# Block 1: which products TensorE takes while the mixers of a layer run

## The chip, the core and the metric

The kernel runs on one core of one Trainium2 chip. The metric is the device time of one execution in microseconds (us); before the change it is 2,830.08 us, the median of three runs (2,829.87 to 2,831.25). The engines are named as in the profile: PE (TensorE, matmuls) with PEld (its weight loads), DVE (VectorE), ACT (ScalarE), POOL (GpSimd) and SP (which issues the DMAs of the weights). Each engine has a queue of its own and takes its instructions strictly in the order of that queue; across engines they wait for each other by semaphores.

## The reference

One sequence of 512 positions and 1,024 features passes two layers of a first block and two of a second. The change touches the first block alone, and there the mixers:

```
h = rms_norm(x);  y = h @ w_in + b_in        # split in columns: mq mk mv mo mi mf | hq hf hi hg | sq sk sv
m_out = head_norm(mlstm(silu(conv(mq, mk)), mv, mi, mf)) * sigmoid(mo)
h_out = head_norm(hgrn2(hq, hf, hi)) * silu(hg)
s_out = swa_sink_attention(rope(norm(sq)), rope(norm(sk)), sv, sinks)
x = x + concat(m_out, h_out, s_out) @ w_out
x = x + square(relu(rms_norm(x) @ w_up)) @ w_down
x = x + sigmoid(rms_norm(x) @ w_ple_gate) * rms_norm(p @ w_ple_proj)
```

`mlstm` is causal linear attention with exponential gates over 4 heads, `hgrn2` a gated recurrence over 4 heads, `swa_sink_attention` attention over a window of 128 positions with 8 query heads.

## The kernel before, in words

Positions come in four tiles of 128. Every projection is a sum of three products, `hi*hi + hi*lo + lo*hi`, of operands split into two fp32r parts (`mm3`, L176 to L178). I call these "products" below. A product for a position-major group has 256 columns, one for a feature-major group or for the output projection 512. Weights come by DMA into `wr`, ACT casts them to `wh`, DVE subtracts to get `wl` (L136, L137).

A layer's mixers are written in this order in `mixers1`: projections of the attention; the attention (`swa`, four tiles of four pairs of heads); projections for HGRN2 (`feat(0)`, `feat(1)`, `w_hi1`) and for the mLSTM (`w_mv1`; `feat(2)` and `feat(3)`, both from `w_f1`); HGRN2 and the mLSTM; the gates (`w_hg1`, `w_mo1`); then the output projection in three parts, `w_oa1` for the attention's rows, `w_oh1` for HGRN2's, `w_ob1` for the mLSTM's.

That is not the order in which an engine gets them. A scheduler gives each engine the instruction that it takes to be ready first and, among those, the one written earlier; so products that need only the normed input are pulled forward into every gap that the scheduler sees on PE. Inside the stages the following runs on PE besides the products, all in plain fp32:

- attention, per pair of heads: two score matmuls (`score_pair`, L1088; the first waits by an added dependency for the mask-and-max operation that read the pair before), then on DVE the mask and maximum (L583, L585), on ACT an exponential for each head (L586), on PE transposes (L591), on ACT a copy (L594), on PE the product with the values (L598);
- HGRN2: eight levels; DVE computes decays and multiplies (L707 to L716), PE does 32 small matmuls a level (L728 for level 0, L732 for the others), DVE merges the result (`copy_predicated`, L739). Level 7 needs no decay;
- mLSTM, per head: four score matmuls (L855), ACT exponentials (L858, L860), DVE multiplies (L862), and ten matmuls with the values (L867).

After a group of products a sink reads its PSUM bank: for the gates L486 (DVE), for the output projection the add into `x` at L497 (DVE), for `feat` L419 (DVE) and L420 (ACT). Banks for products rotate over three buffers.

Of the kernel before, what the change touches and what calls it, by code (L numbers as in the profile page):

```python
# [61 lines left out]
class Builder:  # L62
    def __init__(self, ctx, tc, d, out, cfg=None):
        self.tc, self.nc, self.d, self.out = tc, tc.nc, d, out
        self.cfg = cfg or {}
        nc = self.nc
# [5 lines left out]
        self.nmm, self.banks, self.late = 0, ("mm",), None  # L72
        self.pend, self.nstart, self.sread = [], 0, None
        xa = cp.tile([P, NF * S], F32, name="x")
# [316 lines left out]
    def mixers1(self, l, mp, act, nxt):  # L391
        nc = self.nc
# [70 lines left out]
        self.tok_group(w, 8, 264, act, mv_sink)  # L463
        feat(2)
        feat(3)
        ctx = ExitStack()
# [13 lines left out]
        for name, off, dst, silu in (("w_hg1", O_HG, gg, True), ("w_mo1", O_MO, gm, False)):  # L480
            w = self.wload(name, l, 8 * 256)
            b = bias(off, 256)

            def gate_sink(t, pt, b=b, dst=dst, silu=silu):
                z = dst[t]
                nc.vector.scalar_tensor_tensor(z, pt, rt[:, t:t + 1], b, ALU.mult, ALU.add)  # L486
                th = self.tmp()[:, 0:256]
                nc.scalar.activation(th, z, AF.Tanh, scale=0.5)
                if silu:
                    nc.vector.scalar_tensor_tensor(th, th, 1.0, z, ALU.add, ALU.mult)  # L490
                    nc.vector.tensor_tensor(z, th, gh[:, 256:512], ALU.mult)
                else:
                    nc.vector.scalar_tensor_tensor(z, th, 1.0, gh[:, 0:256], ALU.add, ALU.mult)
            self.tok_group(w, 8, 256, act, gate_sink)

# [27 lines left out]
    def swa(self, l, mp, sp, ysw, row):  # L523
        nc, tc = self.nc, self.tc
        o = 512
        gq, gk, sinks = row[:, o:o + 64], row[:, o + 64:o + 128], row[:, o + 128:o + 136]
        gqk = sp.tile([P, 64], F32, name="gqk")
        nc.vector.tensor_tensor(gqk, gq, gk, ALU.mult)
# [39 lines left out]
        for t in range(NT):  # L568
# [9 lines left out]
            for j in range(8):  # L578
                f, c1 = j // 2, slice(j, j + 1)
                if j % 2 == 0:  # L580
                    pts = self.score_pair([(qs[f][u:u + 64, tt], qs[4][u:u + 64, k0:k0 + w], None) for u in (0, 64)], w)
                s = sp.tile([P, 256], F32, name="sw_s", tag="sw_s", bufs=3)[:, :w]
                i = nc.vector.tensor_tensor_reduce(s, pts[j % 2], msk, 1.0, -3.0e38, ALU.add, ALU.max, accum_out=mx[:, c1])  # L583
                self.sread = i.ins if hasattr(i, "ins") else i
                nc.vector.scalar_tensor_tensor(mx[:, c1], mx[:, c1], n8[:, c1], nsk[:, c1], ALU.mult, ALU.min)  # L585
# [21 lines left out]
    def hgrn(self, l, mp, yf, yhi):  # L607
        nc = self.nc
# [87 lines left out]
        for lev in range(8):  # L696
# [23 lines left out]
            for hh in range(2):  # L720
                b = hh * 64
                pt = self.ps("S")
                for i in range(2):
                    kk, qq = ops[i]
                    for c in range(NT):
                        o, u = i * 256 + c * 64, c * P
                        if lev == 0:
                            nc.tensor.matmul(pt[0:64, o:o + 64], kk[b:b + 64, u:u + 64], qq[b:b + 64, u + 64:u + 128],  # L728
                                             start=True, stop=True, tile_position=(b, 0))
                            continue  # L730
                        for r in (0, 64):
                            nc.tensor.matmul(pt[r:r + 64, o:o + 64], kk[b:b + 64, u + r:u + r + 64],  # L732
                                             qq[b:b + 64, u + r:u + r + 64], start=True, stop=True, tile_position=(b, r))
                if lev == 0:
# [45 lines left out]
    def mlstm(self, l, mp, sp, yf, yv, yg, fv, fb):  # L780
# [61 lines left out]
        for h in range(4):  # L842
# [8 lines left out]
            for j in range(NT):  # L851
                w = S - j * P
                js = slice(j * P, j * P + P)
                pt = self.ps("ST"[j % 2])[:, :w]
                nc.tensor.matmul(pt, k[b:b + 64, js], q[b:b + 64, j * P:S], start=True, stop=True)  # L855
                W = sp.tile([P, S], F32, name="ml_W", tag="ml_W", bufs=2)[:, :w]
# [226 lines left out]
    def score_pair(self, qk, ws):  # L1083

        nc = self.nc
        pts = [self.ps("S")[:, :ws] for _ in range(2)]
        for u, (q, k, row) in enumerate(qk):
            i = nc.tensor.matmul(pts[u], q, k, start=True, stop=True, tile_position=None if row is None else (row, 0))  # L1088
            if not u and self.sread is not None:
                self.tc.add_manual_dep(i.ins if hasattr(i, "ins") else i, self.sread.name, SYNC, reason="pair")  # L1090
        return pts

    def softmax_pair(self, mp, qk, t, in1s, scale):
# [5 lines left out]
        for pt, in1 in zip(pts, in1s):  # L1099
            s = mp.tile([P, S], F32, name="at_s", tag="at_s", bufs=5)[:, :w]  # L1100
            st = mp.tile([P, 2], F32, name="at_st", tag="at_st", bufs=8)
            i = nc.vector.tensor_tensor_reduce(s, pt, in1, -scale, 3.0e38, ALU.add, ALU.min, accum_out=st[:, 0:1])
            self.sread = i.ins if hasattr(i, "ins") else i
            nc.scalar.activation(s, s, AF.Exp, bias=st[:, 0:1], scale=-1.0, accum_out=st[:, 1:2])
            out.append((s, st[:, 1:2]))
# [459 lines left out]
```

## Time and profile before

| what | value |
|---|---|
| median of three runs | 2,830.08 us |
| profiled execution, its own time | 2,830.73 us |
| its span, first to last instruction | 2,829.0 us |
| mean granted clock of PE | 0.963 |
| busy: PE, DVE, ACT, POOL | 97%, 63%, 42%, 9% |

The clock is given as a share of full speed: 1.00 is 2.4 GHz and 0.50 is 1.2 GHz. The mixers of layer 0 take roughly the span's first 330 us, those of layer 1 roughly 760 to 1,055 us; the rest of each layer, and the second block, is not touched. Times below are of layer 0 unless layer 1 is named.

### The profile page before, as it was taken

How to read it: one execution, taken by the hardware profiler on the slowest of the kernel's cores; microseconds unless marked ns; L12 is line 12 of the kernel's file. 1: busy time of each engine (PE TensorE's matmuls, PEld its weight loads, DVE VectorE, ACT ScalarE, POOL GpSimd, SP SyncE). 2: the span in 40 equal slices, each digit the busy share in tenths (PEclk: the TensorE clock that was granted, in tenths of full speed). 3: DMA queues.
4: the chain of work that ended last, by engine and by line, in shares of the span. 5: the costliest groups of instructions: out<-in, count | busy, mean ns of one | idle time of the engine just before them, and what ended most of it. 6: DMA issues, size and time to landing. Idle time of an engine off the chain costs nothing.

```text
span 2829.0 us, 42855 instructions
## 1 busy us (share of the span) xinstructions
PE 2735.1 (97%) x16360; PEld 2330.5 (82%) x16360; DVE 1777.3 (63%) x3896; ACT 1189.1 (42%) x2372; POOL 252.5 (9%) x630
## 2 busy tenths in 40 slices
PE   8998999999999899999999999999999899999998
PEld 7876887889987678878988786888889788888887
DVE  6476777558756866774873476755454476665555
ACT  4564432335446434222553555432234554542332
POOL 2000100002200001000031310000001410100000
PEclk9995899999999679999999999999999999999999
DMA  4210277333221105862332211223332312133322
GB/s 152 83 54 30 77 258 256 125 104 105 73 82 65 41 32 179 257 219 97 98 99 92 66 51 58 90 89 101 101 102 72 113 39 85 39 104 97 90 88 77
DMA packets 87644, 285.59 MB, mean 101 GB/s; under 512 B 10972, under 2 KB 15132, under 8 KB 87440
## 3 DMA queue, kind: packets, MB, share of 16 engines
q1 hardware_dynamic: 81280, 266.49, 29.4%
q0 software_dynamic: 5872, 16.35, 2.2%
q8 instruction: 128, 2.10, 0.3%
q14 instruction: 76, 0.62, 0.1%
q10 hardware_dynamic: 288, 0.03, 0.0%
HBM read 280.69 MB, written 2.14 MB: 100 GB/s over the span
## 4 chain that ended last, share of the span: by engine, by line
PE 75%; DVE 10%; DMA 8%; ACT 3%; issue 2%; POOL 2%; SPq 0%; DVEq 0%; ACTq 0%; POOLq 0%
PE ps_mm L176 12%; PE ps_mm L177 12%; PE ps_mm L178 12%; DMA wm<-w_mod 6%; PE ps_T L176 5%; PE ps_T L177 5%; PE ps_T L178 5%; PE ps_S L176 5%; PE ps_S L178 5%; PE ps_S L177 5%; PE ps_S L1088 3%; DVE wm L1031 2%; PE ps_o L1134 1%; PE ps_T L1128 1%; PE ps_T L867 1%
## 5 line engine op out<-in xcount | busy, mean ns | idle before, releaser
L136 ACT CAST wh<-wr 128x1024 fp32r<-128x1024 f32 (+4 forms) x414 | 407.1, 987 | 682.8 <-PE ps_mm L177 247.4
L137 DVE TENSOR_TENSOR wl<-wr,wh 128x1024 fp32r<-128x1024 f32 (+4 forms) x414 | 472.5, 1143 | 306.9 <-ACT wh L136 300.3
L177 PE MATMUL ps_mm<-slotA,wh 128*128 128x512 f32 (+1 forms) x632 | 226.0, 360 | 4.6 <-DVE slotA L137 2.6
L176 PE MATMUL ps_mm<-slotA,wh 128*128 128x512 f32 (+1 forms) x632 | 225.2, 362 | 1.1 <-ACT slotA L316 0.7
L178 PE MATMUL ps_mm<-slotA,wl 128*128 128x512 f32 (+1 forms) x632 | 225.0, 358 | 0.0
L176 PE MATMUL ps_mm<-wh,slotA 128*128 128x256 f32 (+3 forms) x688 | 208.1, 303 | 0.0
L178 PE MATMUL ps_mm<-wh,slotA 128*128 128x256 f32 (+3 forms) x688 | 205.9, 300 | 0.0
L177 PE MATMUL ps_mm<-wl,slotA 128*128 128x256 f32 (+3 forms) x688 | 204.4, 298 | 0.0
L136 ACT CAST m_h<-tmp 128x512 fp32r<-128x512 f32 (+1 forms) x122 | 71.3, 587 | 212.3 <-DVE tmp L910 175.8
L1031 DVE CUSTOM_DVE_ANT_0 wm<-wm,sc 128x1024 f32<-128x1024 f32 x96 | 117.4, 1224 | 68.2 <-DMA wm<-w_mod 67.7
L176 PE MATMUL ps_mm<-slotB,wh 128*128 128x512 f32 (+1 forms) x408 | 141.8, 354 | 4.5 <-ACT slotB L136 3.3
L176 PEld LDWEIGHTS ps_mm<-wh,slotA 128*128 128x128 f32 x688 | 131.6, 192 | 12.2 <-issue 9.5
L177 PEld LDWEIGHTS ps_mm<-slotA,wh 128*128 128x128 f32 x632 | 121.8, 193 | 24.1 <-DVE slotA L137 4.1
L177 PE MATMUL ps_mm<-slotB,wh 128*128 128x512 f32 (+1 forms) x408 | 141.6, 348 | 0.0
L178 PE MATMUL ps_mm<-slotB,wl 128*128 128x512 f32 (+1 forms) x408 | 140.3, 345 | 0.0
L178 PEld LDWEIGHTS ps_mm<-wh,slotA 128*128 128x128 f32 x688 | 131.1, 191 | 7.5 <-issue 6.9
L176 PEld LDWEIGHTS ps_mm<-slotA,wh 128*128 128x128 f32 x632 | 120.8, 193 | 18.3 <-ACT slotA L316 0.9
L178 PEld LDWEIGHTS ps_mm<-slotA,wl 128*128 128x128 f32 x632 | 121.4, 192 | 17.3 <-issue 1.7
L177 PEld LDWEIGHTS ps_mm<-wl,slotA 128*128 128x128 f32 x688 | 131.2, 191 | 5.0 <-issue 4.6
L176 PE MATMUL ps_S<-m_h,wh 128*128 128x512 f32 (+1 forms) x355 | 129.6, 365 | 2.7 <-DVE yacc L944 2.4
L178 PE MATMUL ps_S<-m_h,wl 128*128 128x512 f32 (+1 forms) x355 | 129.2, 364 | 0.0
L177 PE MATMUL ps_S<-m_l,wh 128*128 128x512 f32 (+1 forms) x355 | 129.2, 364 | 0.0
(635 smaller groups left out, 7242.4 us busy)
## 6 DMA issues: line engine op xcount, KB each, us to landing
wr<-w_up SPq DMA_DIRECT2D x152, 512.0 KB, 3.8
wm<-w_mod SPq DMA_DIRECT2D x96, 512.0 KB, 4.6
wr<-w_dn SPq DMA_DIRECT2D x64, 512.0 KB, 4.0
wr<-w_dn SPq DMA_DIRECT2D x32, 384.0 KB, 3.1
wr<-w_dn SPq DMA_DIRECT2D x32, 320.0 KB, 2.8
wr<-w_f SPq DMA_DIRECT2D x16, 512.0 KB, 3.8
wr<-w_pg SPq DMA_DIRECT2D x16, 512.0 KB, 3.8
wr<-w_t SPq DMA_DIRECT2D x12, 512.0 KB, 4.7
```

Source lines behind the costliest of these rows:

```text
L136: nc.scalar.copy(hi, src)
L137: nc.vector.tensor_tensor(lo, src, hi.bitcast(F32), ALU.subtract)
L176: nc.tensor.matmul(out, ah, bh, start=i == 0, stop=False)
L177: nc.tensor.matmul(out, ah, bl, start=False, stop=False)
L178: nc.tensor.matmul(out, al, bh, start=False, stop=i == n - 1)
L867: nc.tensor.matmul(po[:, t * 66:t * 66 + 66], Ps[j][:, (t - j) * P:(t - j) * P + P], yv[j][:, h, :], start=j == 0, stop=j == t)
L1031: nc.vector.tensor_tensor_reduce(w, w, self.sc, 1.0, 0.0, ALU.mult, ALU.add, accum_out=self.mod[l][:, j:j + 1])
L1088: i = nc.tensor.matmul(pts[u], q, k, start=True, stop=True, tile_position=None if row is None else (row, 0))
L1128: nc.tensor.transpose(tp[:, c * P:c * P + P], s[:, c * P:c * P + P], self.ident)
L1134: nc.tensor.matmul(po[u * 64:u * 64 + 64], v(c, u), pT[:, c * P:c * P + P], start=c == 0, stop=c == t, tile_position=(0, u * 64))
```

## The change

Four groups of products get a place in PE's queue behind an instruction of the mixers (an "anchor"), by a context of the framework (`issue_after`): every PE instruction recorded inside it is queued behind the anchor. The anchors are the PE instructions that the diff stores:

- `feat(2)`, `feat(3)` behind the score matmul of the first pair of the attention's last tile;
- the gate of HGRN2 (`w_hg1`) behind the last matmul of level 0, that of the mLSTM (`w_mo1`) behind the last of level 3;
- the first half of `w_oa1` behind level 6, its second half behind the last score matmul of the mLSTM's head 0.

No instruction is added, removed or resized, and no semaphore wait is asked for: the anchor is on the same engine. POOL's and SP's queues keep their order; PE's, DVE's and ACT's change, since the scheduler lays out everything around the new places, and only inside the two layers' mixers.

```diff
-        feat(2)
-        feat(3)
+        for g in (2, 3):
+            with self.tc.issue_after(self.anchor["swa", NT - 1]):
+                feat(g)
...
-            self.tok_group(w, 8, 256, act, gate_sink)
+            with self.tc.issue_after(self.anchor["level", 0 if silu else 3]):
+                self.tok_group(w, 8, 256, act, gate_sink)
...
         for g in range(2):
-            self.feat_group(self.wload("w_oa1", l * 2 + g, 4 * 512), 4, 4, act, sink, 4 * g)
+            with self.tc.issue_after(self.anchor["head", 0] if g else self.anchor["level", 6]):
+                self.feat_group(self.wload("w_oa1", l * 2 + g, 4 * 512), 4, 4, act, sink, 4 * g)
...
+                    self.anchor.setdefault(("swa", t), self.anchor["pair", None])
...
+                            m = nc.tensor.matmul(pt[0:64, o:o + 64], kk[b:b + 64, u:u + 64], qq[b:b + 64, u + 64:u + 128],
+                                                 start=True, stop=True, tile_position=(b, 0))
+                            self.anchor["level", lev] = m.ins
...
+                self.anchor["head", h] = m.ins
...
+            self.anchor["pair", row] = i.ins
```

PE's queue in layer 0 where the attention passes from its tile 1 to tile 2. Before, with the products of `w_f1` (L176 to L178) around the pairs (L1088 scores, L1144 the row that scales a tile's output, L598 values, L591 transposes):

```order
L177 MATMUL ps_mm<-slotA,wh 128x512
L1088 MATMUL ps_S<-sw_q_765,slotB 128x256
L1144 MATMUL ps_T<-ident,tmp 128x128 x4
L1088 MATMUL ps_S<-sw_q_765,slotB 128x256
L598 MATMUL ps_o<-sw_pT,ysw_205 64x128 x2
L598 MATMUL ps_o<-sw_pT,ysw_206 64x128 x2
L591 MATMUL ps_T<-ident,sw_s 128x128 x4
L178 MATMUL ps_mm<-slotA,wl 128x512
```

Now, at the same pairs (lines are 5 to 9 higher):

```order
L1096 MATMUL ps_S<-sw_q_765,slotB 128x256 x2
L603 MATMUL ps_o<-sw_pT,ysw_205 64x128 x2
L603 MATMUL ps_o<-sw_pT,ysw_206 64x128 x2
L1153 MATMUL ps_T<-ident,tmp 128x128 x4
L596 MATMUL ps_T<-ident,sw_s 128x128 x6
L1096 MATMUL ps_S<-sw_q_765,sw_q_751 128x256 x2
L603 MATMUL ps_o<-sw_pT,ysw_206 64x128 x2
L603 MATMUL ps_o<-sw_pT,ysw_207 64x128 x2
L596 MATMUL ps_T<-ident,sw_s 128x128 x2
L1096 MATMUL ps_S<-sw_q_765,sw_q_758 128x256 x2
```

From the last product of `w_mv1` to the anchor no product stands between the pairs any more; the 96 of `w_f1` that stood there, and at the start of the tile after it, all come behind the anchor.

PE's queue in layer 0 from HGRN2's level 3 on. Before, the small matmuls of the levels (L732) follow each other, with a few transposes of the mLSTM (L811, L810) and its first scores (L855):

```order
L178 MATMUL ps_mm<-slotA,wl 128x512
L678 MATMUL ps_o<-yhi_1326,hg_kt_1508 128x128
L732 MATMUL ps_S<-tmp 64x64 x40
L811 MATMUL ps_T<-ident,ml_W 128x4
L810 MATMUL ps_T<-ident,ml_P_1853 128x4
```

Now products of the gates stand between two levels (L738), 32 to 36 at a time:

```order
L176 MATMUL ps_mm<-wh,slotA 128x256
L177 MATMUL ps_mm<-wl,slotA 128x256
L738 MATMUL ps_S<-tmp 64x64 x32
L178 MATMUL ps_mm<-wh,slotA 128x256
L176 MATMUL ps_mm<-wh,slotA 128x256
```

Before, the product that opens the first of these two pieces is the last one ahead of the end of the mLSTM; now all 192 of the two gates and all 96 of `w_oa1` come between level 0 and that end.

DVE's queue in layer 0. Before, the adds of `w_oa1` into `x` (L497) stand among the operations of HGRN2's levels (L715, L716 multiply, L739 merges) and of the mLSTM's gates (L796):

```order
L716 TENSOR_TENSOR tmp<-tmp,slotB 128x8x32
L497 TENSOR_TENSOR x<-x,ps_mm 128x512
L715 TENSOR_TENSOR tmp<-tmp,slotB 128x16x16
L716 TENSOR_TENSOR tmp<-tmp,slotB 128x16x16
L796 SCALAR_TENSOR_TENSOR ml_W<-ml_W 4x512
L137 TENSOR_TENSOR wl<-wr,wh 128x1024
```

Now three of the eight (L499) stand just ahead of the mLSTM's first product of scores and weights (L870), the others behind it:

```order
L838 SCALAR_TENSOR_TENSOR ml_W<-yf_1833,ml_cw,ml_W 128x512 x3
L499 TENSOR_TENSOR x<-x,ps_mm 128x512 x2
L843 SCALAR_TENSOR_TENSOR yf_1833<-ml_W 128x512
L137 TENSOR_TENSOR wl<-wr,wh 128x1024
L499 TENSOR_TENSOR x<-x,ps_mm 128x512
L870 TENSOR_TENSOR ml_P_2313<-ps_S,ml_W 128x512
```

The third of them reads the 36th product of `w_oa1`, so what follows on DVE waits for that.

## Rows read from the trace of the kernel before

**Rows 1.** The page of the profile: its span, and the granted clock in 40 slices.

```profile
span 2829.0 us, 42855 instructions
PEclk9995899999999679999999999999999999999999
```

**Rows 2.** Windows by stage: microseconds, busy time and count per engine, clock, DMA.

```profile
core 0: us, PE busy (x) PEld busy (x) DVE busy (x) ACT busy (x) POOL busy (x), PEclk, DMA share, GB/s
112.20:144.10 31.90, 31.90 (x175) 23.06 (x173) 15.42 (x46) 16.16 (x35) 1.79 (x3) 1.00 0.36 118
144.10:162.60 18.50, 18.50 (x143) 15.20 (x143) 9.25 (x33) 9.75 (x25) 0.00 (x0) 1.00 0.09 30
162.60:249.20 86.60, 75.27 (x763) 61.74 (x761) 79.63 (x176) 48.29 (x88) 6.24 (x11) 0.82 0.17 56
249.20:291.50 42.30, 38.85 (x143) 31.41 (x144) 17.44 (x57) 16.13 (x44) 3.54 (x6) 0.50 0.05 13
949.00:1021.00 72.00, 64.25 (x427) 51.55 (x427) 43.83 (x111) 29.79 (x70) 7.58 (x10) 0.50 0.05 16
```

**Rows 3.** Windows of PE: length, busy (instructions), granted clock, DMA share and GB/s.

```profile
216.00:219.00 3.00, 1.15 (x32) 0.95 0.01 3
219.00:222.00 3.00, 0.43 (x8) 0.50 0.71 208
297.00:300.00 3.00, 2.99 (x16) 0.96 0.00 0
```

**Rows 4.** Timeline of PE: start, length, product; 512 columns, 256 columns, 512 at half clock.

```profile
112.29 0.40 PE L176 MATMUL ps_mm<-slotA,wh 128*128 128x512 f32 x1
112.52 0.39 PE L177 MATMUL ps_mm<-slotA,wh 128*128 128x512 f32 x1
...
157.04 0.28 PE L176 MATMUL ps_mm<-wh,slotA 128*128 128x256 f32 x1
157.16 0.28 PE L177 MATMUL ps_mm<-wl,slotA 128*128 128x256 f32 x1
...
295.55 0.63 PE L176 MATMUL ps_mm<-slotA,wh 128*128 128x512 f32 x1
295.98 0.63 PE L177 MATMUL ps_mm<-slotA,wh 128*128 128x512 f32 x1
```

**Rows 5.** Timeline of PE in the attention: transposes, PV and scores of one pair.

```profile
124.64 0.66 PE L591 MATMUL ps_T<-ident,sw_s 128*128 128x128 f32 x4
...
130.05 0.66 PE L598 MATMUL ps_o<-sw_pT,ysw 128*64 128x128 f32 x8
...
131.00 0.70 PE L1088 MATMUL ps_S<-sw_q,sw_q 64*128 64x256 f32 x4
```

**Rows 6.** Groups by line on ACT, 112.2 to 162.6 us: busy, mean ns, idle before.

```profile
L586 ACT ACTIVATE sw_s<-sw_s,sw_mx,sw_r 128x256 f32<-128x256 f32 x18 | 10.8, 598 | 8.6 <-DVE sw_mx L585 8.6
L594 ACT COPY sw_pT<-ps_T 128x512 f32<-128x512 f32 x8 | 4.7, 582 | 9.9 <-PE ps_T L591 9.9
```

**Rows 7.** Timeline of PE: products of the HGRN2 levels, and the wait before one.

```profile
202.56 0.97 PE L732 MATMUL ps_S<-tmp 64*64 64x64 f32 x32
...
221.57 1.12 PE L732 MATMUL ps_S<-tmp 64*64 64x64 f32 x16 [3.92 <-DVE tmp L716]
...
239.93 1.97 PE L732 MATMUL ps_S<-slotB 64*64 64x64 f32 x32
```

**Rows 8.** Groups by line and form on DVE, 162.6 to 249.2 us.

```profile
L137 DVE TENSOR_TENSOR wl<-wr,wh 128x1024 fp32r<-128x1024 f32 x8 | 9.7, 1218 | 0.1
L497 DVE TENSOR_TENSOR x<-x,ps_mm 128x512 f32<-128x512 f32 x8 | 5.2, 674 | 0.1
L486 DVE SCALAR_TENSOR_TENSOR gg<-ps_mm,rt,brow 128x256 f32<-128x256 f32 x1 | 0.5, 486 | 0.3 <-PE ps_mm L178 0.3
```

**Rows 9.** Timeline of DVE: first operation of HGRN2, first product of the mLSTM.

```profile
162.61 0.64 DVE L634 SCALAR_TENSOR_TENSOR tmp<-slotB 128x512 f32<-128x512 f32 x1
...
249.18 0.69 DVE L862 TENSOR_TENSOR ml_P<-ps_S,ml_W 128x512 f32<-128x512 f32 x1 [1.03 <-ACT ml_W L860]
```

More of the change, by code (lines that the diff above doesn't have):

```diff
@@ L72, in __init__ @@
         self.nmm, self.banks, self.late = 0, ("mm",), None
-        self.pend, self.nstart, self.sread = [], 0, None
+        self.pend, self.nstart, self.sread, self.anchor = [], 0, None, {}
         xa = cp.tile([P, NF * S], F32, name="x")
@@ L526, in swa @@
         gq, gk, sinks = row[:, o:o + 64], row[:, o + 64:o + 128], row[:, o + 128:o + 136]
+        self.anchor = {}
         gqk = sp.tile([P, 64], F32, name="gqk")
@@ L581, in swa @@
                     pts = self.score_pair([(qs[f][u:u + 64, tt], qs[4][u:u + 64, k0:k0 + w], None) for u in (0, 64)], w)
+                    self.anchor.setdefault(("swa", t), self.anchor["pair", None])
                 s = sp.tile([P, 256], F32, name="sw_s", tag="sw_s", bufs=3)[:, :w]
                 i = nc.vector.tensor_tensor_reduce(s, pts[j % 2], msk, 1.0, -3.0e38, ALU.add, ALU.max, accum_out=mx[:, c1])
-                self.sread = i.ins if hasattr(i, "ins") else i
+                self.sread = i.ins
                 nc.vector.scalar_tensor_tensor(mx[:, c1], mx[:, c1], n8[:, c1], nsk[:, c1], ALU.mult, ALU.min)
@@ L727, in hgrn @@
                         if lev == 0:
-                            nc.tensor.matmul(pt[0:64, o:o + 64], kk[b:b + 64, u:u + 64], qq[b:b + 64, u + 64:u + 128],
-                                             start=True, stop=True, tile_position=(b, 0))
+                            m = nc.tensor.matmul(pt[0:64, o:o + 64], kk[b:b + 64, u:u + 64], qq[b:b + 64, u + 64:u + 128],
+                                                 start=True, stop=True, tile_position=(b, 0))
+                            self.anchor["level", lev] = m.ins
                             continue
                         for r in (0, 64):
-                            nc.tensor.matmul(pt[r:r + 64, o:o + 64], kk[b:b + 64, u + r:u + r + 64],
-                                             qq[b:b + 64, u + r:u + r + 64], start=True, stop=True, tile_position=(b, r))
+                            m = nc.tensor.matmul(pt[r:r + 64, o:o + 64], kk[b:b + 64, u + r:u + r + 64],
+                                                 qq[b:b + 64, u + r:u + r + 64], start=True, stop=True, tile_position=(b, r))
+                            self.anchor["level", lev] = m.ins
                 if lev == 0:
@@ L854, in mlstm @@
                 pt = self.ps("ST"[j % 2])[:, :w]
-                nc.tensor.matmul(pt, k[b:b + 64, js], q[b:b + 64, j * P:S], start=True, stop=True)
+                m = nc.tensor.matmul(pt, k[b:b + 64, js], q[b:b + 64, j * P:S], start=True, stop=True)
+                self.anchor["head", h] = m.ins
                 W = sp.tile([P, S], F32, name="ml_W", tag="ml_W", bufs=2)[:, :w]
@@ L1088, in score_pair @@
             i = nc.tensor.matmul(pts[u], q, k, start=True, stop=True, tile_position=None if row is None else (row, 0))
+            self.anchor["pair", row] = i.ins
             if not u and self.sread is not None:
-                self.tc.add_manual_dep(i.ins if hasattr(i, "ins") else i, self.sread.name, SYNC, reason="pair")
+                self.tc.add_manual_dep(i.ins, self.sread.name, SYNC, reason="pair")
         return pts
@@ L1102, in softmax_pair @@
             i = nc.vector.tensor_tensor_reduce(s, pt, in1, -scale, 3.0e38, ALU.add, ALU.min, accum_out=st[:, 0:1])
-            self.sread = i.ins if hasattr(i, "ins") else i
+            self.sread = i.ins
             nc.scalar.activation(s, s, AF.Exp, bias=st[:, 0:1], scale=-1.0, accum_out=st[:, 1:2])
```

## The prediction, made before the changed kernel ran

> **What bounds the kernel now.** I read the clock first, since PE is busy for 97% of the span and a busy PE says nothing until its clock is known. The 40 slices of the page show two dents, one in each layer's mixers [rows 1]. Then I cut layer 0's mixers into stages [rows 2]. The attention from its tile 2 on, 112.2 to 144.1 us, runs at full clock with PE never idle; so does the stretch to 162.6. HGRN2, 162.6 to 249.2, has a mean clock of 0.82, and the mLSTM after it, to 291.5, runs wholly at 0.50, which is 1.2 GHz instead of 2.4. Narrow windows give the edge: 0.95 at 216 to 219 us, 0.50 at 219 to 222, 0.96 again at 297 to 300 [rows 3]. Just before the fall PE had run out of products and was idle for more than half of 216 to 219; in 219 to 222 it was busy for 0.43 us, and a level's matmul at 221.57 waited 3.92 us for DVE [rows 3, 7]. It comes back when the products of `w_oh1` fill PE. So some 297 - 219 = 78 us of layer 0 run at half clock, and layer 1 does the same (949 to 1,021 us, 0.50) [rows 2].
>
> Who waits for whom differs by stage. In the attention PE is full, and its products set the pace: a 512-column product starts every 0.23 us (0.228 over a long run of them), a 256-column one every 0.12, at half clock 0.43 and about 0.24 [rows 4]. In HGRN2 DVE is the bound: 79.6 of 86.6 us busy. In the mLSTM PE is: 38.85 of 42.3 us, with DVE at 17.4 and ACT at 16.1 [rows 2]. There a doubled clock would halve what bounds the stage. The stages meet at two operations of DVE, HGRN2's first at 162.61 and the mLSTM's first product at 249.18 [rows 9]; I price the time up to each.
>
> **The change, part by part.** Nothing is added or removed; each part takes time from one stage and gives it to another. I go through one layer and double the sum.
>
> *A, the attention up to HGRN2's first operation.* 93 products of `w_f1` (all like the first two there [rows 4]) leave 112.2 to 144.1, where the anchor stands at the end: 93 x 0.228 = 21.2 us. What is left of the 31.9 us is 10.7 us of PE for five pairs. That is the least the five pairs can take. The most is that nothing overlaps: a pair takes 1.8 us on PE (0.59 + 0.59 + 0.63, as far as one start is from the next in such pairs [rows 5]), an exponential 0.60 and a copy 0.58 on ACT [rows 6], and about 0.65 for the mask on DVE, 3.6 us, or 18 for five. I take 14, since `sw_s` has three buffers and two pairs can overlap. The anchor then falls at 126 instead of 144, -18 us. From there to DVE's first HGRN2 operation the queue now has 72 products of `w_f1` ahead of the sink that DVE takes before it, 72 x 0.228 = 16.4, in place of 3 of them and some 96 gate products (18.5 us of PE before, 3 x 0.228 and 96 x 0.12 off, leaves 6.3 of other work). 126 + 16.4 + 6.3 = 148.7; with 3 us for waits of the last pairs 151.7 against 162.6: **-11 us**. If the five pairs need 18 and the rest another us, -6; if they need the 10.7, -15 at the outside.
>
> On the five pairs the Trainium skill bears, "TensorE: Matmul & The Clock Gate", section "Part 4: PE-mode transpose": full clock is said not to engage for transposes, as they do not count as busy PE in the same way. The attention without products is to a third transposes. No row of before shows the attention alone, so neither is borne out; by the page this stretch falls to 1.2 GHz, which is the second rival.
>
> *B, HGRN2 up to the mLSTM's first product.* DVE is the bound, so its operations count. Before 249.18 it loses five adds of `w_oa1` into `x` (5 x 0.674) and three subtractions for `wl` (3 x 1.218), 7.0 us, and gets three gate sinks from ahead of HGRN2 (3 x 0.486), one `wl` (1.22) and one `feat` add (as L497, 0.67), 3.35 [rows 8]: -3.7. DVE idles 7.0 us of the stage, and the moved operations can fill some: -2. Against it stands a new wait. The third add stands ahead of the mLSTM's first product in DVE's queue and needs the 36th product of `w_oa1`, which cannot begin before level 6 ends: at most 36 x 0.228 = 8.2 us, of which DVE has some work of its own to cover; I take 5. The gate products come in pieces of 32 to 36 between levels, 32 x 0.12 = 3.84 us a piece. They stand in PE's queue while DVE computes the next level's decays, which are longer; but where a level's operands are ready first, its 32 matmuls wait behind them, and at full clock these take 0.97 instead of 1.97 us [rows 7]. Sum **0 us** (-0.7 by these numbers), bounds -5 (no stall at all) and +10 (the stall in full, and two levels behind half a piece).
>
> This is where the clock is decided: between 219 and 249 us PE now has products in the gaps. Before, products mixed with levels held 1.00 up to 216, and products alone brought it back at 297.
>
> *C, the mLSTM, 42.3 us.* PE's own 38.85 us at half clock are 19.4 at full. Now 60 products of `w_oa1` (96 less the 36) stand in it as well, 60 x 0.228 = 13.7. Floor 33 us. If all of it stays at half clock, 38.85 + 60 x 0.43 = 64.6. I take 37, the floor with one short fall: **-5 us**. Bounds -12 (30 us: DVE's and ACT's 16 to 17 us lie within it, and some of the 60 products fall into the gaps ahead) and +3; +22 if the clock stays down, which is the first rival.
>
> *D, the tail.* From 291.5 to 297 the products of `w_oh1` run at 0.43 apiece until the clock returns; at full clock those 5.5 us are 2.8 shorter. **-2 us**, bounds -2.7 and 0.
>
> SP's and POOL's queues keep their order, and weights come early (DMA share 0.05 to 0.36 in these stages [rows 2]), so a transfer costs nothing; if a buffer of `wh` is freed later by a gate, the next weights still have 60 us.
>
> Sum: -11 + 0 - 5 - 2 = -18 us a layer, -36 us for two. Against the profiled execution's own 2,830.73 us (span 2,829.0, the rest around it) that is 2,794.7; the median of before is 0.65 lower, so 2,794 us.
>
> **The rivals.**
>
> *First, slower: the clock does not come back.* Half-size pieces of products with pauses between, then an mLSTM of small matmuls, leave PE at 1.2 GHz from level 3 on. Stage C is then 64.6 us (+22), pieces of 32 products cost 7.7 us instead of 3.84 and the levels wait for them (+5), and A still gives -11: +16 a layer, 2,863 us. For it: PE was busy 38.85 of 42.3 us in the mLSTM and stayed at 0.50, so being busy with that work does not raise the clock. Against it: the new 60 products in C are of the kind that held 1.00 in the attention. It decides once C exceeds 42.3 + 11 = 53 us with B at 0, that is when some two thirds of C, (53 - 33)/(64.6 - 33), run at half clock.
>
> *Second, a smaller gain: the clock falls in the attention.* Without products its five pairs run at 1.2 GHz; their 10.7 us of PE become 21.4 instead of the 14 I took, +7.4, and about 15 products of `w_f1` at half clock add 3. A is then -1, the sum -8 a layer, 2,815 us. For it: the matmuls of a pair leave gaps on PE, and in 216 to 219 a PE busy for 1.15 of 3 us lost its clock [rows 3]. Against it: the pairs overlap, and PE is busy for 10.7 of 14 us.
>
> *Third, no change:* the full clock is won, but each wait behind a piece of products gives it back: B at its +10, A at -6, C at -5. Sum -3 a layer or less: 2,825 to 2,836.
>
> *Fourth, more:* no stall in B (-5), C at 30 (-12), A at -13: -32 a layer, 2,768 us.
>
> That the change doesn't do what it says is not among them: the order shows the products behind their anchors.
>
> **How the numbers follow.** Main case 0.55, first rival 0.14, second 0.16, third 0.08, fourth 0.07. A run tells some 0.2% from no change, 5.7 us. Main, second and fourth are faster by more: 0.78; the third is within it: 0.08; the first is slower: 0.14. The main case's own range is 2,775 to 2,812; the second rival and the nearer halves of the third and fourth widen it to 2,765 to 2,832. The first rival, and the far end of the fourth, are left out.
>
> **What would show it.** Right: a granted clock near 1.00 from 219 us through the mLSTM; HGRN2's first operation on DVE at 150 to 154 us; the mLSTM stage at 33 to 42 us; in HGRN2 a length near 86 us with DVE still the bound. A wrong: a clock of 0.50 somewhere in 112 to 126 us, or the anchor later than 130. B wrong: DVE idle for over 8 us before the third add of `w_oa1`, or level matmuls waiting behind products with DVE waiting for the level. C wrong: a clock of 0.50 for most of the mLSTM. The prediction is wrong as a whole if the clock stays up and the time does not fall, for then PE's clock was not what bound the mLSTM.

## The result, and the profile after

The changed kernel takes 2,799.82 us (median of four runs, 2,797.01 to 2,807.06) against 2,830.05 before (now four runs): a ratio of 0.9896, 95% interval 0.9877 to 0.9915, or 30 us less. The profiled execution is the slowest of the four, 2,807.06 us.

The page's span and clock, to be held against [rows 1]: the two dents of before go down to 5 and 6; now a single 8 is left in each layer.

```profile
span 2805.0 us, 42838 instructions
PEclk9989999999998999999999999999999999999999
```

Windows of the changed kernel in layer 0 (columns as in [rows 2]). The first five follow the stages, the last four are stretches that turned out to matter.

```profile
112.20:127.00 14.80, 11.29 (x68) 6.39 (x64) 8.47 (x34) 9.71 (x26) 1.17 (x2) 0.77 0.40 132
127.00:154.82 27.82, 27.82 (x150) 20.43 (x151) 11.77 (x37) 14.21 (x32) 0.61 (x1) 1.00 0.11 39
154.82:238.29 83.47, 69.44 (x811) 59.76 (x810) 75.56 (x173) 48.30 (x90) 6.74 (x11) 0.88 0.13 45
238.29:271.03 32.74, 32.74 (x173) 24.33 (x172) 19.67 (x51) 17.75 (x44) 3.28 (x5) 1.00 0.20 65
271.03:293.29 22.26, 20.25 (x100) 15.69 (x100) 21.23 (x67) 6.60 (x11) 0.56 (x1) 0.92 0.15 50
...
115.00:125.00 10.00, 8.39 (x44) 4.98 (x44) 4.64 (x19) 6.45 (x18) 0.61 (x1) 0.66 0.33 110
160.00:175.00 15.00, 2.30 (x10) 1.61 (x9) 14.05 (x39) 12.45 (x20) 0.00 (x0) 0.63 0.10 35
175.00:185.00 10.00, 10.00 (x76) 8.23 (x75) 7.89 (x22) 6.08 (x11) 0.00 (x0) 0.53 0.01 2
180.00:270.00 90.00, 88.67 (x894) 74.33 (x891) 72.53 (x163) 46.53 (x103) 6.31 (x9) 0.98 0.16 54
```

From 180 to 270 us, where before had 0.50 from 219 on, the clock is 0.98, with levels, products and mLSTM mixed. Two new stretches lie at half clock: one in the attention that has lost its products (115 to 125 us, 0.66), and one from 164 to 184 us, which begins in a stretch where PE has almost nothing to do (2.30 us of work in 160 to 175).

DVE's timeline at the two operations of [rows 9]:

```profile
154.82 0.64 DVE L639 SCALAR_TENSOR_TENSOR tmp<-slotB 128x512 f32<-128x512 f32 x1
...
237.69 0.68 DVE L499 TENSOR_TENSOR x<-x,ps_mm 128x512 f32<-128x512 f32 x1
238.29 0.68 DVE L870 TENSOR_TENSOR ml_P<-ps_S,ml_W 128x512 f32<-128x512 f32 x1
```

HGRN2 starts 7.8 us earlier (154.82 against 162.61) and the mLSTM 10.9 (238.29 against 249.18). The third add of `w_oa1` (L499), which I took for a stall of 5 us, waits for nothing. I close a layer's mixers with a mark, the second add into `x` over 256 columns, where both kernels do the same again: 309.75 before and 293.29 after in layer 0, 1,038.11 and 1,010.75 in layer 1. That is -16.5 and, with those taken off, -10.9 us. The rows of layer 1, before and then after (the second row holds three adds, the first at 1,010.41):

```profile
1038.11 0.41 DVE L497 TENSOR_TENSOR x<-x,ps_mm 128x256 f32<-128x256 f32 x1
```

```profile
1010.41 1.08 DVE L499 TENSOR_TENSOR x<-x,ps_mm 128x256 f32<-128x256 f32 x3 [0.59 <-PE ps_mm L178]
```

The same from PE's side, before and then after, from 100 us (layer 0) and 816.4 or 800 us (layer 1) to those marks:

```profile
100.00:309.75 209.75, 194.55 (x1400) 156.26 (x1397) 145.16 (x378) 103.66 (x214) 11.63 (x20) 0.81 0.15 49
...
816.40:1038.11 221.71, 207.74 (x1468) 167.04 (x1468) 152.32 (x402) 114.29 (x234) 14.21 (x22) 0.82 0.16 52
```

```profile
100.00:293.29 193.29, 173.73 (x1393) 136.84 (x1392) 143.49 (x377) 104.22 (x214) 12.36 (x20) 0.92 0.16 54
...
800.00:1010.75 210.75, 186.08 (x1467) 147.60 (x1465) 152.18 (x404) 113.96 (x232) 13.57 (x22) 0.90 0.17 55
```

A mean clock of 0.81 over 209.75 us is 0.19 x 2 x 209.75 = 80 us at half clock. So read, half clock goes from 80 + 80 to 31 + 42 us, and PE's idle time (length less busy) from 15.2 + 14.0 to 19.6 + 24.7. If a microsecond at half clock costs half of one and an idle one a whole, that is -43.5 + 15.1 = -28 us; the marks say -27.4. I use this account, lost time = idle + half of the half clock, in all that follows.

### The profile page after: what moved, and what is told of

The parts are those of the page before. It is cut to its first block, busy times and chain, and to the rows that moved or that the text cites. A ratio compares the mean times of both kernels' runs of the same rounds, so it can differ in the third digit from the quotient of the medians.

```text
span 2805.0 us, 42838 instructions
## 1 busy us (share of the span) xinstructions
PE 2693.3 (96%) x16360; PEld 2291.4 (82%) x16360; DVE 1775.7 (63%) x3896; ACT 1189.6 (42%) x2372; POOL 252.2 (9%) x630
## 4 chain that ended last, share of the span: by engine, by line
PE 75%; DVE 9%; DMA 8%; ACT 3%; POOL 2%; issue 2%; SPq 0%; DVEq 0%; ACTq 0%; POOLq 0%
PE ps_mm L176 12%; PE ps_mm L177 12%; PE ps_mm L178 12%; DMA wm<-w_mod 7%; PE ps_T L176 5%; PE ps_T L177 5%; PE ps_T L178 5%; PE ps_S L176 5%; PE ps_S L177 5%; PE ps_S L178 5%; PE ps_S L1096 3%; DVE wm L1039 2%; PE ps_o L1143 1%; PE ps_T L1137 1%; DVE wl L137 1%
## 5 line engine op out<-in xcount | busy, mean ns | idle before, releaser
L176 PE MATMUL ps_mm<-slotA,wh 128*128 128x512 f32 (+1 forms) x632 | 224.7, 361 | 1.2 <-ACT slotA L316 0.7
L178 PE MATMUL ps_mm<-slotA,wl 128*128 128x512 f32 (+1 forms) x632 | 225.3, 358 | 0.0
L176 PE MATMUL ps_mm<-wh,slotA 128*128 128x256 f32 (+3 forms) x688 | 209.5, 305 | 0.0
L178 PE MATMUL ps_mm<-wh,slotA 128*128 128x256 f32 (+3 forms) x688 | 206.4, 300 | 0.0
L176 PE MATMUL ps_mm<-slotB,wh 128*128 128x512 f32 (+1 forms) x408 | 141.5, 353 | 3.8 <-ACT slotB L136 3.4
L176 PEld LDWEIGHTS ps_mm<-wh,slotA 128*128 128x128 f32 x688 | 132.5, 193 | 12.2 <-issue 9.1
L178 PE MATMUL ps_mm<-slotB,wl 128*128 128x512 f32 (+1 forms) x408 | 140.1, 344 | 0.0
L178 PEld LDWEIGHTS ps_mm<-wh,slotA 128*128 128x128 f32 x688 | 132.3, 192 | 7.2 <-issue 6.6
L176 PEld LDWEIGHTS ps_mm<-slotA,wh 128*128 128x128 f32 x632 | 120.4, 192 | 20.3 <-issue 2.8
L178 PEld LDWEIGHTS ps_mm<-slotA,wl 128*128 128x128 f32 x632 | 121.4, 192 | 18.1 <-issue 2.5
L176 PE MATMUL ps_S<-m_h,wh 128*128 128x512 f32 (+1 forms) x355 | 129.5, 365 | 2.9 <-DVE yacc L952 2.6
L178 PE MATMUL ps_S<-m_h,wl 128*128 128x512 f32 (+1 forms) x355 | 129.3, 364 | 0.0
```

Source lines behind the costliest of these rows:

```text
L176: nc.tensor.matmul(out, ah, bh, start=i == 0, stop=False)
L178: nc.tensor.matmul(out, al, bh, start=False, stop=i == n - 1)
```

## The experiments

Ten of the twelve kernels are variants of the anchors; two add work. The last two columns are the change against before, over both layers, in the profiled execution: by the account (windows of 2 us from 100 to 330 and from 800 to 1,070 us; useless products added at 0.228 and 0.12 us) and by layer 1's mark, which is good to about 1 us. A profiled execution is one of the runs and need not be the median: `hg_free`'s took 2,797.7 us, `spread2`'s 2,827.6.

| kernel | median, us | ratio to before (95%) | idle, us | half clock, us | account | mark |
|---|---|---|---|---|---|---|
| before | 2,830 to 2,832 | 1 | 29 | 160 | 0 | 0 |
| changed | 2,799.8 | 0.9896 (0.9877 to 0.9915) | 44 | 72 | -29 | -27.4 |
| `f_only` | 2,822.4 | 0.9970 (0.9958 to 0.9981) | 29 | 150 | -5 | -8.5 |
| `no_f` | 2,810.8 | 0.9922 (0.9909 to 0.9934) | 51 | 55 | -31 | -23.9 |
| `g_only` | 2,809.0 | 0.9923 (0.9909 to 0.9936) | 49 | 61 | -30 | -22.3 |
| `o_only` | 2,833.6 | 1.0011 (1.0002 to 1.0020) | 48 | 136 | +6 | +4.5 |
| `hg_free` | 2,806.1 | 0.9904 (0.9892 to 0.9917) | 34 | 82 | -34 | -30.6 |
| `spread2` | 2,820.8 | 0.9968 (0.9956 to 0.9979) | 42 | 120 | -8 | -5.5 |
| `f3_only` | 2,805.5 | 0.9912 (0.9899 to 0.9926) | 48 | 65 | -29 | -26.1 |
| `late2` | 2,807.4 | 0.9913 (0.9900 to 0.9927) | 42 | 72 | -32 | -24.9 |
| `late3` | 2,787.9 | 0.9850 (0.9837 to 0.9864) | 38 | 55 | -44 | -41.0 |
| `late3_hg` | 2,800.7 | 0.9897 (0.9881 to 0.9914) | 39 | 65 | -38 | -35.1 |
| `late3_warm` | 2,797.8 | 0.9882 (0.9867 to 0.9897) | 17 | 24 | -57 | -44.4 |
| `dummy` | 2,855.8 | 1.0082 (1.0067 to 1.0097) | 20 | 99 | +4 | +9.9 |

The account gives the right sign each time and the size to within 8 us (some 13 for `late3_warm`). It mostly overstates the gain; where PE waits at half clock, the account charges the same time for both.

**The change taken apart.** `f_only` keeps the anchors of `w_f1` alone, `no_f` all the others.

```diff
-            with self.tc.issue_after(self.anchor["level", 0 if silu else 3]):
-                self.tok_group(w, 8, 256, act, gate_sink)
+            self.tok_group(w, 8, 256, act, gate_sink)
...
-            with self.tc.issue_after(self.anchor["head", 0] if g else self.anchor["level", 6]):
-                self.feat_group(self.wload("w_oa1", l * 2 + g, 4 * 512), 4, 4, act, sink, 4 * g)
+            self.feat_group(self.wload("w_oa1", l * 2 + g, 4 * 512), 4, 4, act, sink, 4 * g)
```

> Only the products of w_f1 are anchored (behind the last attention tile's first score matmul); gates and w_oa1 as before. Clock theory (the gain of the whole change comes from PE's clock in HGRN2's tail and the mLSTM): HGRN2 starts some 8 us earlier a layer, but the gates and w_oa1 are used up early again and the mLSTM runs at 0.50 as before, so at most half of the 30 us: 2,812 to 2,830 us. Early-start theory (the gain comes from DVE's earlier HGRN2 start, the clock is a by-product): all of it, about 2,800 us, whatever the clock of the mLSTM.

```diff
-            with self.tc.issue_after(self.anchor["swa", NT - 1]):
-                feat(g)
+            feat(g)
```

> The gates and w_oa1 are anchored, the products of w_f1 stay in the attention as before. Clock theory: mLSTM at or near full clock, its stage and the tail some 8 us a layer shorter, no fall of the clock in the attention: 2,800 to 2,818 us. HGRN2 starts at most 5 us earlier than before (the gates' 96 products ahead of it are gone). Early-start theory: little or nothing, 2,822 to 2,830 us.

`f_only` takes 9 us off, `no_f` 21. HGRN2 starts as early in `f_only` as in the changed kernel (155.1 us), but its clock from 203 to 290 us is 0.65, and its mLSTM, from the start of DVE's first product to that of its last, takes 35.3 us (before 37.3, changed 32.7). In `no_f` the clock holds 1.00 in the attention (105 to 150 us) and from 183 to 270. The windows of `f_only`, then of `no_f`:

```profile
203.00:290.00 87.00, 77.09 (x544) 61.59 (x535) 58.58 (x139) 34.80 (x76) 6.74 (x10) 0.65 0.12 38
```

```profile
105.00:150.00 45.00, 44.39 (x268) 32.15 (x264) 24.34 (x72) 25.37 (x52) 1.78 (x3) 1.00 0.26 86
183.00:270.00 87.00, 84.36 (x877) 70.13 (x876) 68.74 (x154) 43.72 (x97) 5.96 (x10) 1.00 0.16 50
```

The early-start theory falls: the early start without the clock brings 9 us of the 30. But `no_f` isn't the clock by itself. With the gates' 96 products gone from ahead of it, HGRN2 starts early there too, 6.5 us earlier than before in layer 0 (and some 5 more in layer 1), where I had expected at most 5 a layer. Its row in layer 0:

```profile
156.15 0.64 DVE L638 SCALAR_TENSOR_TENSOR tmp<-slotB 128x512 f32<-128x512 f32 x1
```

So 9 and 21 make 30 although both runs hold most of the early start, and they are not the shares of two causes (by the marks the two add up to 32 against 27). What compares better is `f_only` with `no_f`: they win about as much at HGRN2's start, to within 1 us or so a layer, have 150 and 55 us at half clock, and end 12 us apart. How the rest divides was not settled.

**Gates or `w_oa1`?** `g_only` has the gates' anchors alone, `o_only` those of `w_oa1` alone; each edit is the second diff above with one half of the first.

> Only the two gates are anchored (behind levels 0 and 3); w_f1 and w_oa1 have no anchor. With the gates late, w_oa1 is queued behind them of its own accord, so PE's queue in HGRN2 and the mLSTM is nearly that of the kernel with gates and w_oa1 anchored. Theory (what counts is that products last into the mLSTM, by whichever group): as that kernel, 2,806 to 2,815 us. Rival (it is the anchors of w_oa1 at level 6 and head 0 that carry the gain): at most a third of it, 2,823 to 2,831 us.

> Only w_oa1 is anchored; the gates fill the start of HGRN2 as before, and the levels run without a product. Theory (clock): the clock falls in the levels, from 190 us or so in layer 0, comes back with the products of w_oa1 after level 6; the mLSTM runs at full clock, and DVE bounds the levels anyway, so most of the mLSTM's gain stays: 2,808 to 2,822 us. Rival (the w_oa1 products only push the end of PE's work back, since nothing shortens HGRN2): 2,826 to 2,836 us.

`g_only` is `no_f` within their intervals: once the gates come late, `w_oa1` queues behind them by itself, and its anchors carry nothing that shows. `o_only` is slower than before, by 0.1%, which I had given to the rival. Its levels run without products at half clock, the mLSTM gets its clock back, and still takes 39.2 us, since now it has to carry `w_oa1`:

```profile
180.00:240.00 60.00, 43.07 (x523) 36.21 (x524) 54.25 (x125) 26.12 (x50) 2.31 (x4) 0.52 0.08 28
241.31:280.51 39.20, 39.20 (x195) 29.70 (x194) 18.02 (x38) 19.48 (x47) 3.05 (x5) 0.93 0.13 41
```

My theory was too simple there: 24 us less at half clock (160 to 136, 12 in the account) do not pay for 18 us more of idle PE. Products that are moved leave a hole where they were.

**The clock by itself.** `dummy` moves nothing, but issues the 96 products of `w_oa1` a second time, at the change's places, unread: useless work. Against the kernel before:

```diff
-            self.feat_group(self.wload("w_oa1", l * 2 + g, 4 * 512), 4, 4, act, sink, 4 * g)
+            w = self.wload("w_oa1", l * 2 + g, 4 * 512)
+            self.feat_group(w, 4, 4, act, sink, 4 * g)
+            with self.tc.issue_after(self.anchor["head", 0] if g else self.anchor["level", 6]):
+                self.feat_group(w, 4, 4, act, lambda m, pt, sl: None, 4 * g)
```

> The kernel before (no product moved) with the 96 products of w_oa1 issued a second time, at the places where the change puts w_oa1 (behind level 6 and behind head 0's scores), into PSUM banks that nobody reads: pure extra work of 22 us a layer at full clock. Clock theory: the mLSTM, from its first product on DVE to its last, takes 37 us before; with some 30 to 40 of these extra products (7 to 9 us) in it, it gets shorter all the same, 28 to 34 us at a granted clock above 0.9; the rest of the extra products stands behind it and makes the whole 10 to 25 us longer than before. Filling theory (the clock doesn't matter to the chain of the mLSTM, only when products run): 44 us or more.

Groups of PE by line in the mLSTM of layer 0, from the start of DVE's first product to that of its last: window and groups of before (249.18 to 286.46), then of `dummy` (242.56 to 276.67).

```profile
249.18:286.46 37.28, 33.95 (x120) 26.51 (x120) 17.18 (x56) 15.82 (x43) 3.05 (x5) 0.50 0.05 15
...
L867 PE MATMUL ps_T<-yv,ml_P 128*128 128x66 f32 x60 | 14.0, 424 | 0.0
L855 PE MATMUL ps_S<-yf,yf 64*128 64x512 f32 (+1 forms) x12 | 8.9, 897 | 2.2 <-DVE ml_P L862 2.2
```

```profile
242.56:276.67 34.11, 34.11 (x177) 24.64 (x177) 15.90 (x36) 17.65 (x45) 3.07 (x5) 0.97 0.10 33
...
L875 PE MATMUL ps_T<-yv,ml_P 128*128 128x66 f32 x60 | 7.7, 275 | 0.0
L177 PE MATMUL ps_mm<-slotA,wh 128*128 128x512 f32 x16 | 6.9, 432 | 0.0
...
L862 PE MATMUL ps_S<-yf,yf 64*128 64x256 f32 (+1 forms) x14 | 6.4, 536 | 0.0
```

With 48 products more in it (16 on each of three lines, 11 us) the stage is 3 us shorter, and the same 60 rows of matmuls take 275 ns each instead of 424. The 3 us are not the clock's, though. In the kernel before, DVE takes sixteen multiplications for HGRN2's output (3.22 us, L776) just ahead of its last two products, and PE waits 2.73 us for those two; in `dummy` the sixteen (L783) come behind. The rows of before, then of `dummy`:

```profile
282.86 3.22 DVE L776 SCALAR_TENSOR_TENSOR gg<-slotB,hg_r,gg 128x64 f32<-128x64 f32 x16
286.00 0.75 DVE L862 TENSOR_TENSOR ml_P<-ps_T,ml_W 128x384 f32<-128x384 f32 x2
...
286.60 4.53 PE L867 MATMUL ps_T<-yv,ml_P 128*128 128x66 f32 x20 [2.73 <-DVE ml_P L862]
```

```profile
276.67 0.29 DVE L870 TENSOR_TENSOR ml_P<-ps_T,ml_W 128x128 f32<-128x128 f32 x1
...
278.34 3.22 DVE L783 SCALAR_TENSOR_TENSOR gg<-slotB,hg_r,gg 128x64 f32<-128x64 f32 x16
```

Less these 3.2 us, the two stages are of about one length, 34.1 us. So at 0.97 the stage took in 11 us of useless work and grew no longer, where PE's idle time (37.28 less 33.95) could have held 3.3 us of it: the rest is the clock's. (The same sixteen lie inside the 37.3 and 35.3 us of before and `f_only` above, and all but two of them outside the changed kernel's 32.7.) In layer 1 it is 37.8 us against 35.3, of which 3.2 are again those multiplications; there the extra work outweighed the clock. The kernel as a whole is 24 us slower than before, for 44 us of useless products. Some 10 of the 24 us stand at layer 1's mark; the rest came behind it, where nothing is added (1,805.0 us from the mark to the end, before 1,790.8), and what took them was not settled. The clock is a cause by itself; what it is worth is less than the time at half clock.

**Where the new holes are.** `hg_free` lets `w_hg1` go without anchor, so that it fills 160 to 175 us.

```diff
-            with self.tc.issue_after(self.anchor["level", 0 if silu else 3]):
+            with nullcontext() if silu else self.tc.issue_after(self.anchor["level", 3]):
```

> As the changed kernel, but the gate w_hg1 has no anchor, so its 96 products (11.5 us) can fill the stretch at 160 to 175 us in which PE stood idle and lost its clock. Clock theory: no 0.50 between 160 and 184 us in layer 0; but DVE bounds that stretch, so only some 0 to 5 us a layer, 2,790 to 2,800 us, and the levels 0 to 3 may lose the clock in turn. Early-start theory: as the changed kernel, 2,797 to 2,807 us.

It takes 2,806 us, no better than the changed kernel; that is the early-start theory's range, though its reason is out by the runs above. HGRN2's stage is 72.8 us instead of 83.5, but its first levels fell instead (half clock from 178 to 204 us), and some 55 products of `w_oa1` were left behind the mLSTM: from DVE's last product of it to the mark 33.4 us, 22.3 in the changed kernel. `spread2` tried to mend both, with `w_mo1` behind level 0 and `w_oa1` behind level 5 and head 1.

> As the changed kernel, but w_hg1 without anchor (it fills the start of HGRN2), w_mo1 behind level 0, and the halves of w_oa1 behind level 5 and behind head 1's scores. Theory (the time goes where PE is idle or at half clock): in the kernel with w_hg1 free the stage HGRN2 was 73 to 78 us, but 55 products of w_oa1 came after the mLSTM and the tail was 33 us; here they stand ahead of its end. HGRN2 76, mLSTM 33, tail 25: 134 us against 138.5 of the changed kernel's layer 0, 2,786 to 2,797 us. Rival (products in HGRN2 and the mLSTM cost DVE as much as they save on PE): 2,797 to 2,808 us as the changed kernel.

It lost most of the gain (2,821 us, slower than either range). PE ran dry at 210 us and had shorter waits from 234 on, where the mLSTM begins; with each came a fall, and the mLSTM took 41.6 us.

**The attention.** `f3_only` anchors feat(3) alone; feat(2) stays in tile 2, where the changed kernel's clock fell.

```diff
-            with self.tc.issue_after(self.anchor["swa", NT - 1]):
+            with self.tc.issue_after(self.anchor["swa", NT - 1]) if g == 3 else nullcontext():
```

> As the changed kernel, but feat(2) has no anchor: 48 products of w_f1 stay in the attention's tile 2, 48 come behind the anchor. Theory (the product-free attention costs a fall of the clock, 7 us or so at half clock, and gains the earlier anchor): no 0.5 to 0.7 in 112 to 126 us, HGRN2's first operation within 2 us of the changed kernel's 154.8, 2,796 to 2,803 us. Rival (every product moved out of the attention is an equal gain): half of the part that w_f1's anchors bring, so 2,803 to 2,808 us.

The fall in the attention is gone and HGRN2 starts at 155.6 us, both as expected. Yet 2,805 us is the rival's range; the interval (2,801 to 2,809 us on that chip) touches the other's. So it shows no gain from holding the clock in the attention. It can't price the fall by itself, since 48 products moved back with it and its interval overlaps the changed kernel's.

**A version that beats both.** In the changed kernel the attention's own last scores stand behind products: DVE's last mask operations wait 4.48 us for a score matmul, at 150.22.

```profile
150.22 0.43 DVE L588 CUSTOM_DVE_ANT_0 sw_s<-ps_S,c_swam 128x256 f32<-128x256 f32 x1 [4.48 <-PE ps_S L1096]
```

So the products that come right behind the anchor delay the pairs behind it, and are missing 10 us later. `late2` and `late3` put feat(3) behind the attention's last score matmul; `late3` leaves feat(2) without anchor as well.

```diff
-            with self.tc.issue_after(self.anchor["swa", NT - 1]):
+            with nullcontext() if g == 2 else self.tc.issue_after(self.anchor["pair", None]):
                 feat(g)
```

> As the changed kernel, but feat(3), 48 of the 96 products of w_f1, stands behind the last score matmul of the attention instead of the first one of its last tile, so that it fills the stretch at 160 to 178 us in which PE of the changed kernel had nothing. Theory (time goes where PE is idle or at half clock): HGRN2 starts some 8 us earlier (146 to 148 us in layer 0), the idle of 160 to 175 us is filled by 11 us, the clock of 165 to 180 us holds at least in part; 5 to 10 us a layer less than the changed kernel if nothing is late next: 2,782 to 2,797 us. Rival (DVE bounds HGRN2 and the feat operations now lie in its way): HGRN2's stage grows by what its start gained, 2,797 to 2,807 us.

> As the changed kernel, but feat(2) without anchor (48 products stay in the attention's tile 2, where the changed kernel's clock fell) and feat(3) behind the attention's last score matmul (48 products for the stretch at 160 to 178 us). Theory (idle and half clock): no fall in the attention, and less idle before level 0: 2,782 to 2,797 us. Rival (DVE's chain bounds, see the run with feat(3) alone moved): 2,797 to 2,810 us.

`late3` takes 2,787.9 us, 44 us less than before and 12 less than the changed kernel. Its attention holds 1.00, HGRN2 starts at 149.64, and the levels and the mLSTM are as in the changed kernel (83.5 and 32.7 us):

```profile
112.20:149.64 37.44, 35.93 (x226) 25.49 (x226) 20.91 (x74) 24.04 (x57) 1.79 (x3) 1.00 0.28 89
149.64:233.16 83.52, 70.94 (x816) 60.94 (x815) 76.79 (x173) 48.86 (x92) 6.72 (x11) 0.88 0.14 46
```

`late2`, with feat(2) behind the last tile's first scores, still starts HGRN2 at 154.3 us: its last transposes came behind products of feat(3), and DVE waited 4.31 us for them. Neither step by itself (`f3_only`, `late2`) is enough; 2,807 us, the upper end of its rival's range.

Two more on top of `late3`: `late3_hg` leaves the first two tiles of `w_hg1` without anchor, `late3_warm` issues all of `w_hg1` a second time, unread, ahead of level 0.

```diff
+            if silu:
+                self.tok_group(w, 8, 256, act, lambda t, pt: None)
```

> As the kernel with feat(2) free and feat(3) behind the attention's last score matmul (2,788 us), but the first two of w_hg1's four tiles have no anchor: 48 of its products (5.8 us) can fill what is left of the idle at 152 to 165 us; levels 0 and 1 have fewer. Theory (idle and half clock): some of the 12 us of idle and of the half clock up to 183 us goes, 0 to 5 us a layer: 2,778 to 2,788 us. Rival (the products are then missing where the levels need them): a new fall in the levels or the mLSTM, 2,788 to 2,800 us.

> As the kernel with feat(2) free and feat(3) behind the attention's last score matmul (2,788 us), with the 96 products of w_hg1 issued once more, unread, ahead of level 0: 11.5 us a layer of work that is of no use, in the stretch in which PE had nothing and fell to half clock. If only the lost clock costs there (the stretch is DVE's), the useless work is nearly free and the levels start at full clock: 2,780 to 2,792 us. If PE is the bound over the mixers as a whole, so that idle time of PE costs its length, useless work in it changes nothing but the half clock: the same range. If the products stand in the way of HGRN2's own matmuls: up to 23 us more, 2,795 to 2,811 us.

`late3_hg` (2,801 us, just above its rival's range) went the rival's way: new falls behind holes at 210 us and, in layer 1, at 920 us. `late3_warm` filled the hole and kept the clock there. Windows of `late3`, then of `late3_warm`:

```profile
149.00:175.00 26.00, 14.74 (x94) 10.76 (x93) 23.69 (x58) 19.87 (x31) 3.70 (x7) 0.68 0.12 41
```

```profile
149.00:175.00 26.00, 26.00 (x228) 23.12 (x229) 24.59 (x62) 20.66 (x36) 2.84 (x7) 1.00 0.13 42
```

Layer 0's mark came at 280.9 us, some 7 earlier than in `late3`, with 11.5 us of useless work in it. So in layer 0 the hole and its clock cost more than useless products do. The whole is 10 us slower than `late3` all the same, in the range of the third expectation, but not at the place it named: layer 1's mark is still 3.5 us earlier, and from there to the end the profiled execution took 1,803.9 us, 15 more than `late3`'s. As in `dummy`, what took that time was not settled.

## Why the prediction came out

The forecast was 2,794 us; the measured 2,799.82 lies inside the range and at five sixths of the forecast gain (30.2 of 36). By its steps, in us per layer, read from the profiled execution (the slowest of the four):

| step | predicted | layer 0 | layer 1 |
|---|---|---|---|
| A, to HGRN2's first operation | -11 | -7.8 | -7.4 |
| B, to the mLSTM's first product | 0 | -3.1 | 0.0 |
| C and D, to the mark | -7 | -5.6 | -3.5 |
| sum | -18 | -16.5 | -10.9 |

**A: the anchor came where I put it, what followed took longer.** The anchor ran at 126.91 us, forecast 126: 14.6 us for the five pairs, against my 14. PE's timeline shows how:

```profile
112.96 0.44 PE L596 MATMUL ps_T<-ident,sw_s 128*128 128x128 f32 x2
116.13 0.66 PE L596 MATMUL ps_T<-ident,sw_s 128*128 128x128 f32 x2 [2.74 <-ACT sw_s L591]
116.72 1.23 PE L1096 MATMUL ps_S<-sw_q,slotB 64*128 64x256 f32 x4
...
125.94 0.66 PE L603 MATMUL ps_o<-sw_pT,ysw 128*64 128x128 f32 x8
126.54 0.44 PE L596 MATMUL ps_T<-ident,sw_s 128*128 128x128 f32 x2
126.91 0.70 PE L1096 MATMUL ps_S<-sw_q,slotB 64*128 64x256 f32 x4
127.54 0.50 PE L176 MATMUL ps_mm<-slotA,wh 128*128 128x512 f32 x1
```

A wait of 2.74 us for an exponential, then a clock of 0.50: the mechanism of the second rival did happen (0.66 over 115 to 125 us, 0.50 from 118 to 122; by my own signs A was wrong there), but the anchor came only 0.9 us later than forecast, where I had priced 7.4. That is in part luck: of the five pairs' matmuls with the values, 0.59 us a pair, one pair's ran ahead of the stretch (111.73 us) and another's behind the anchor (130.26), so PE had less to do in it than I took. Two windows of the same stretch show the clock back at 1.00 before a single product had run:

```profile
116.00:118.00 2.00, 1.87 (x8) 0.89 (x10) 1.10 (x5) 1.35 (x6) 0.00 (x0) 0.55 0.68 246
...
124.00:126.00 2.00, 1.57 (x10) 0.76 (x11) 1.28 (x8) 1.80 (x6) 0.00 (x0) 1.00 0.05 12
```
So the rule that I cited from the Trainium skill ("TensorE: Matmul & The Clock Gate", section "Part 4: PE-mode transpose") agrees with the fall, but this trace doesn't show that transposes were its cause: the return in the same mix of transposes and scores speaks against it, and the idle PE just before the fall is as good a cause.

The term that was mis-sized is the stretch behind the anchor: 25.7 us by my sum (72 products, 6.3 of other work, 3 of waits), 27.9 measured, so that HGRN2 started 0.8 us after the 154 that I had named as the latest. The 72 products were right; the sink that DVE takes before HGRN2 (L419) stands right behind the 72nd:

```profile
151.91 0.40 PE L178 MATMUL ps_mm<-slotA,wl 128*128 128x512 f32 x1
...
152.50 0.69 DVE L419 TENSOR_TENSOR yf<-ps_mm,R 128x512 f32<-128x512 f32 x1
```

But from the anchor to the end of the 72nd are 25.4 us, and 72 x 0.228 are 16.4: the attention's own matmuls among the products took 9.0 us of a PE that was never idle, not 6.3. Each pair had to wait its turn there, as the 4.48 us above show. `late3`, with feat(3) behind the pairs, started HGRN2 5.2 us earlier.

**B: the balance of DVE was right, the stall was not.** DVE's operations, 79.6 us before, are 75.6, -4.1 against my -3.7. The stall of the third add did not occur: level 6 was done early enough for 36 products (the 36th started at 236.19 us, the add at 237.69). Without it my sum would have been -5.7, where -3.1 and 0.0 were measured; so my 0 came near by two misses that offset each other. What I had not seen is the hole: I counted the gate sinks that move, but not that without the gates PE has nothing between the attention and level 0, and falls. With that hole filled (`late3_warm`) the stage is 80.8 and 87.6 us in the two layers, without (`late3`) 83.5 and 89.7. No rival held this. One row I misread, without weight in the sum: the profile lists each of these plain fp32 matmuls as two (64 rows for a level's 32), so the 0.97 and 1.97 us for 32 rows are half a level.

**C and D: right in kind.** The granted clock from 238 to 271 us is 1.00 and the mLSTM is PE's, 32.7 us busy of 32.7. I had named 33 to 42 for the wider stage; to the end of the last matmul with the values it is 34.5 us, before 41.95. From the mLSTM's first product to the mark it went from 60.6 to 55.0 us. The gain is short of my 7 by 1.4 in layer 0 and 3.5 in layer 1; why layer 1 gained less was not tested.

The first rival (the clock stays down) is out: 0.98 from 180 to 270 us. The third (all is given back) and fourth as well. (The fourth's -32 a layer is 2,766 us, not the 2,768 that I wrote.) Of the second, the mechanism was there and its price was not.

What is left between the marks' -27.4 us and the profiled execution's -23.7 lies outside the mixers, where nothing was changed. The clearest case is at the same wait of both kernels, before and after in turn:

```profile
1194.00:1204.00 10.00, 8.94 (x39) 6.76 (x38) 9.59 (x16) 3.47 (x4) 0.00 (x0) 1.00 0.76 249
```

```profile
1170.00:1180.00 10.00, 8.13 (x32) 6.34 (x31) 7.55 (x12) 3.22 (x4) 0.00 (x0) 0.89 0.81 258
```

PE waits there 1.06 us for DVE in the one execution and 1.87 in the other, and in the second the clock falls behind it.

## What to carry to other kernels

Look at the granted clock before the busy share: a PE that was busy for 92% of a stage sat at 1.2 GHz through all of it, and 48 products of no use, with which the clock was 0.97, made that stage no longer in layer 0. Independent products are a stock that can be spent once; add up PE's idle time and half of its half clock over the whole region, because a group moved into one hole opens another, and spend the stock where PE would stand empty, not ahead of matmuls that another engine waits for.

## What the hardware did that I had not expected

- Full clock came back without any dense products, in the attention, at 122 to 124 us, while in the mLSTM of before PE was busy without a gap from 251 to 283 us and the clock stayed at 0.50 throughout. What the two mixes differ in for the clock was not settled.

```profile
251.00:283.00 32.00, 32.00 (x118) 0.50 0.06 17
```

- The same wait outside the mixers, 1.87 us long in the changed kernel's execution and 1.06 in the other, was followed by a fall in the one and not in the other (0.89 and 1.00 above). The single runs of the changed kernel spread over 2,797 to 2,807 us, those of before over 2,830 to 2,831, and in the sixteen runs of it that go with `f3_only` over 2,828 to 2,834. In the changed kernel's four runs the mean granted clock goes with the time, from 0.982 at the fastest to 0.978 at the slowest; among `f3_only`'s four it does not.
